# Crossed halves of a complex state scan, multiplied by VectorE out of PSUM instead of exchanged by transfers

## The chip, the cores and the metric

The kernel runs on one core of a Trainium2 chip. A core has five engines with their own instruction streams: TensorE (PE in the profile; its weight loads are listed as PEld), VectorE (DVE), ScalarE (ACT), GpSimd (POOL) and SyncE (SP). Each executes its stream in order and waits on semaphores that other engines and transfers set. Transfers (DMAs) are issued by SP, ACT or POOL, each into its own queue, and are carried out by 16 DMA engines that all queues share. SBUF is the on-chip memory of 128 partitions, PSUM the memory into which TensorE writes; it has 8 banks of 128 x 512 numbers in float32.

The metric is the device time of one execution in microseconds (us), as the median of the timed runs.

## The reference

One decoder layer on 1024 tokens of width 1024: a SwiGLU feed-forward half step, a mixer, a second feed-forward half step and a final norm, with shifts, scales and gates that come from a conditioning vector. The change lies in the mixer, in the part that the reference calls `s5_mixer`:

```python
lam_bar = jnp.exp(lam * dt)
b_bar = ((lam_bar - 1) / lam)[..., None] * b
bu = jnp.einsum('gpc,bsgc->bsgp', b_bar, uf.astype(jnp.complex64))
a = jnp.broadcast_to(lam_bar, bu.shape)
_, states = lax.associative_scan(_ssm_combine, (a, bu), axis=1)
y = jnp.einsum('gcp,bsgp->bsgc', c, states).real + d_skip * uf
y = jax.nn.gelu(y)
y = y * jax.nn.sigmoid(y @ glu_w + glu_b)
```

There are 32 groups of 16 channels, each with 64 complex states; `lam_bar` is a complex decay for each state. The mixer's other half is a gated convolution of three taps; both halves are normed and go through one output projection.

## The kernel before

Large products are done in float32 as three passes on TensorE (a high part and a low part of either factor; the product of the two low parts is dropped), by the helper `mm3`: three matmuls of 128 x 512. Weights arrive as tiles `raw` over SP's queue (sums of two blocks get their second summand by a transfer from POOL's queue); ACT casts each to its high part and DVE subtracts to get the low part, into tiles `w`, of which there are four. The large projections use a seven-product scheme (`seven`), each of whose seven steps has 8 calls of `mm3`, so a projection has 56. Three of its PSUM sums (A, B, C), each as a pair, live in six banks (`mm_ps`); DVE adds them up, and a bank comes free when DVE or ACT has read it.

**The order of the work.** The program is written as one stream in which `mm3` advances a clock by one tick, and side work is put on the clock: `clock.after(n, fn)` runs `fn` n ticks later. A planner then sets the order within each engine from this, so that two neighbours of the text may change places; in the stage of the batches below (`InOrder.strict`) the order is that of the text.

**The scan in complex numbers.** The time axis of 1024 is folded: 8 steps (TAU) are taken together by matrix products, and 128 folded steps (J) remain for the scan. The 32 groups are worked through in NB = 8 batches of GB = 4. For a batch a tile of 128 x 512 holds the real parts of the 64 states in partitions 0 to 63 and the imaginary parts in 64 to 127, with 4 x 128 folded steps along the row. Since the decay has a phase, the state is turned back by an angle before the scan, so that the scan itself has a real factor (`r8`), and turned forward after it. A turn is a complex product: `co` (cosines) times the tile, plus `si` (sines with signs) times the tile with its halves exchanged. Per batch (all in the mixer's stage):

- `state_in`: PE forms `px`, the input to the states (weights `mi` times `u`), in a bank of the six, and `py`, the direct part of the output (weights `mk` times `u`), in one of two further banks (`sm_ps`). ACT copies `px` to `X` (sX in the profile), and the helper `swapped` writes `X` with its halves exchanged into a tile (swx) by two transfers on ACT's queue.
- `state_scan`, 12 ticks later: DVE forms co times X and si times swx, adds them, runs four scans, and forms si times X and co times X.
- `state_swap`, at tick 20: two more transfers exchange the halves of si times X (into swz).
- `state_end`, at tick 31: DVE adds swz.
- `outputs`, at tick 34: PE adds the states' part (weights `mo`) to `py`, ACT applies the Gelu (yg), and ACT's queue stores the result (`y_d`).

A batch starts every 18 ticks, so that before the change two batches overlap: `outputs` of batch b at 34 lies two ticks ahead of `state_in` of batch b + 2 at 36.

`u_load` fetches a batch's u on ACT's queue from `u_d`, where the input projection's four parts have been stored by SP; `in_loads`, `mo_load`, `co_load` and `si_load` fetch the weights and tables on SP's queue. `mi`, `mk` and `mo` have one buffer, `u`, `co` and `si` two. After the scan `y_back` reads the results back as rows of channels, `x_again` fetches the residual stream, `split_g` splits the results for the gate `glu`, and `w_out` is the output projection; its first half needs `oa`, the normed convolution (`outnorm`), its second the gated results.

Beside the scan run the seven-step projections that the convolution needs, `cv0` and `cv2`, and `b`: 168 ticks in all. Their sums, the three-tap convolution (`conv`, five instructions for 128 channels) and the weights' low parts are DVE's other work in this stage.

**The batches' weights** are formed much earlier, in the first feed-forward half step (`ssm_batch`, as side work): DVE forms `cl` and `bl` by `comb` (two products with broadcast factors and a sum), PE forms `kp` and transposes `bl` into `tp`, ACT copies that to `mi`, and SP stores the tiles to DRAM (`mo_d`, `co_d`, `si_d`, `mk_d`, `mi_d`). These tiles come from one pool of four buffers (`bt`), so that the next batch's first instructions (`bb`) wait until stores have landed. Before the change `bl` has its columns in the order group, channel, step, so that DVE writes them at a stride of 8 numbers.

Of the kernel before, what the change touches and what calls it, by code (L numbers as in the profile page):

```python
# [13 lines left out]
F32 = mybir.dt.float32  # L14
# [7 lines left out]
P = 128  # L22
# [20 lines left out]
NB = 8  # L43
# [188 lines left out]
def hymba_layer(ctx: ExitStack, tc, x_d, xt_d, wm1_d, wmod_d, gu1_d, gs1_d, ds10_d, ds11_d, wl1_d, win_d, wcvb_d, wout_d, glu_d, gu2_d, gs2_d, wd2_d, ds20_d, ds21_d, ds22_d, wl2_d, cols_d, cond_d, lam_d, bc_d, out_d):  # L232
# [29 lines left out]
    def ps(name):  # L262
        return mm_ps.tile([P, HALF], F32, tag="mm", name=name)
# [942 lines left out]
    def ssm_batch(b):  # L1206
        bp = bps[0]
        gs = slice(b * GB, (b + 1) * GB)
        prm = ssm["prm"]
        bb = bp.tile([P, 2, GB, CH], F32, tag="bb", name=f"bb{b}")  # L1210
        q = tuple(ssm["q"][:, i, gs].unsqueeze(2).to_broadcast([P, GB, CH]) for i in range(2))
        cmul(bp, bb[:], prm[:, 0:2], q, [GB, CH], f"bb{b}")
        p1, p2, e1, e2 = ssm["tabs"]
        yield

        def bt(name):
            return bp.tile([P, 576], F32, tag="bt", name=name, bufs=4)

        def comb(dst, n, lam, src, op, nm):

            t = bt(nm)[:, : GB * n * CH].rearrange("p (g n c) -> p g n c", g=GB, n=n)
            la = [a[:, 0:n, gs].rearrange("p n g -> p g n").unsqueeze(3).to_broadcast([P, GB, n, CH]) for a in lam]
            sc = [a.unsqueeze(2).to_broadcast([P, GB, n, CH]) for a in src]
            V.tensor_tensor(out=dst, in0=la[0], in1=sc[0], op=ALU.mult)
            yield
            V.tensor_tensor(out=t, in0=la[1], in1=sc[1], op=ALU.mult)
            yield
            V.tensor_tensor(out=dst, in0=dst, in1=t, op=op)
            yield

        cl = bt(f"cl{b}")
        cl4 = cl[:].rearrange("p (g n c) -> p g n c", g=GB, n=9)
        yield from comb(cl4, 9, (p1, p2), (prm[:, 2], prm[:, 3]), ALU.add, f"clt{b}")
        SP.dma_start(mo_d[b].rearrange("p (g m) -> p g m", g=GB), cl4[:, :, 1:9, :].rearrange("p g n c -> p g (n c)"))
        if b + 1 < NB:
            prm_load(b + 1)
        bl = bt(f"bl{b}")
        bl4 = bl[:, :512].rearrange("p (g c n) -> p g n c", g=GB, n=8)
        yield from comb(bl4, 8, (e1, e2), (bb[:, 0], bb[:, 1]), ALU.add, f"blt{b}")

        def v3(a):
            return a[:, :512].rearrange("p (g m i) -> p g m i", g=GB, m=8)

        bs = [a[:, gs, :].unsqueeze(2).to_broadcast([P, GB, 8, 16]) for a in ssm["base"]]
        st = [ssm["step"][:, i, :, gs].rearrange("p m g -> p g m").unsqueeze(3).to_broadcast([P, GB, 8, 16]) for i in range(2)]
        r, t = bt(f"rot{b}"), bt(f"rott{b}")
        V.tensor_tensor(out=v3(r), in0=st[0], in1=bs[0], op=ALU.mult)
        yield
        V.tensor_tensor(out=v3(t), in0=st[1], in1=bs[1], op=ALU.mult)
        yield  # L1250
        V.tensor_tensor(out=r[:, :512], in0=r[:, :512], in1=t[:, :512], op=ALU.add)
        yield

        kp = sm([CH, 512], f"kp{b}")
        for g in range(GB):
            T.matmul(
                kp[:, g * P : (g + 1) * P], lhsT=bl4[:, g, 7, :], rhs=cl4[:, g, 0:8, :].rearrange("p n c -> p (n c)"), start=True, stop=True
            )
        tp = sm([P, 512], f"tp{b}")
        for g in range(GB):  # L1260
            T.transpose(tp[:, g * P : (g + 1) * P], bl[:, g * P : (g + 1) * P], ident[:])
        A.activation(t[64:128, :512], r[64:128, :512], AF.Copy, scale=-1.0)
        for half in (slice(0, 64), slice(64, 128)):
            SP.dma_start(co_d[b, half], r[0:64, :512])
        SP.dma_start(si_d[b, 0:64], r[64:128, :512])
        SP.dma_start(si_d[b, 64:128], t[64:128, :512])
        yield
        kc = bt(f"kc{b}")
        kc3 = kc[:CH, :512].rearrange("p (g m) -> p g m", g=GB)
        A.copy(kc[:CH, :512], kp[:])  # L1270
        mi = bt(f"mi{b}")
        A.copy(mi[:, :512], tp[:])
        yield
        for g in range(GB):
            V.scalar_tensor_tensor(
                out=kc3[:, g, 0:CH], in0=ident[:CH, :CH], scalar=ssm["lam"][:CH, 3, b * GB + g : b * GB + g + 1], in1=kc3[:, g, 0:CH], op0=ALU.mult, op1=ALU.add
            )
        for g in range(GB):
            SP.dma_start(mk_steps(b * GB + g), kc3[:, g, :].unsqueeze(1).to_broadcast([CH, TAU, P]))
        SP.dma_start(mi_d[b], mi[:, :512])  # L1280
        yield

    def gate1():
# [278 lines left out]
    def u_groups(b):  # L1562

        half = slice(b % 2 * GB * CH, (b % 2 + 1) * GB * CH)
        return u_d[b // 2][half, :].rearrange("(g c) (t j) -> (c t) g j", g=GB, t=TAU)
# [4 lines left out]

    def u_load(b):
        held["u", b] = sp.tile([P, GB, J], F32, tag="u", name=f"ub{b}", bufs=2)
        A.dma_start(held["u", b][:], u_groups(b))

    def co_load(b):
        held["co", b] = ld("co", co_d[b], b, 2)
# [1 line left out]
    def si_load(b):  # L1578
        held["si", b] = ld("si", si_d[b], b, 2)
# [5 lines left out]
    def mo_load(b):  # L1585
        held["mo", b] = ld("mo", mo_d[b], b)

    def swapped(src, b, nm):

        sw = sp.tile([P, GB * P], F32, tag=nm, name=f"{nm}{b}")  # L1590
        A.dma_start(sw[0:64], src[64:128])
        A.dma_start(sw[64:128], src[0:64])
        return sw

    def state_in(b):

        u, mi, mk = (held.pop((n, b)) for n in ("u", "mi", "mk"))
        px = ps(f"px{b}")
        py = held["py", b] = sm([P, GB * J], f"py{b}")
        for g in range(GB):  # L1600
            q = slice(g * P, (g + 1) * P)
            T.matmul(px[:, q], lhsT=mi[:, q], rhs=u[:, g, :], start=True, stop=True)
        X = held["X", b] = sp.tile([P, GB * J], F32, tag="sX", name=f"sX{b}")
        A.copy(X[:], px[:])
        held["sw", b] = swapped(X, b, "swx")
        for g in range(GB):
            q = slice(g * P, (g + 1) * P)
            T.matmul(py[:, q], lhsT=mk[:, q], rhs=u[:, g, :], start=g == 0, stop=False, skip_group_check=True)
        if b + 2 < NB:
            clock.after(3, lambda: u_load(b + 2))  # L1610
        if b + 1 < NB:
            clock.after(3, lambda: in_loads(b + 1))

    def state_scan(b):

        co, si, X, sw = held["co", b], held["si", b], held.pop(("X", b)), held.pop(("sw", b))
        V.tensor_tensor(out=X[:], in0=co[:], in1=X[:], op=ALU.mult)
        V.tensor_tensor(out=sw[:], in0=si[:], in1=sw[:], op=ALU.mult)
        V.tensor_tensor(out=X[:], in0=X[:], in1=sw[:], op=ALU.add)
        for g in range(GB):  # L1620
            q = slice(g * P, (g + 1) * P)
            V.tensor_tensor_scan(
                out=X[:, q], data0=r8[:, b * GB + g : b * GB + g + 1].to_broadcast([P, J]), data1=X[:, q], initial=0.0, op0=ALU.mult, op1=ALU.add
            )
        V.tensor_tensor(out=si[:], in0=X[:], in1=si[:], op=ALU.mult)
        V.tensor_tensor(out=co[:], in0=X[:], in1=co[:], op=ALU.mult)

    def state_swap(b):
        held["sw", b] = swapped(held.pop(("si", b)), b, "swz")
        if b + 2 < NB:  # L1630
            clock.after(13, lambda: si_load(b + 2))

    def state_end(b):
        co = held["co", b]
        V.tensor_tensor(out=co[:], in0=co[:], in1=held.pop(("sw", b))[:], op=ALU.add)

    def outputs(b):
        st, py, mo = (held.pop((n, b)) for n in ("co", "py", "mo"))
        for g in range(GB):
            late, early = slice(g * P + 1, (g + 1) * P), slice(g * P, (g + 1) * P - 1)  # L1640
            T.matmul(py[:, late], lhsT=mo[:, g * P : (g + 1) * P], rhs=st[:, early], start=False, stop=True, skip_group_check=True)
        yg = sp.tile([P, GB * J], F32, tag="yg", name=f"yg{b}")
        A.activation(yg[:], py[:], AF.Gelu_apprx_tanh)
        A.dma_start(y_groups(b), yg[:].rearrange("p (g j) -> p g j", g=GB))
        if b + 1 < NB:
            clock.after(3, lambda: mo_load(b + 1))
        if b + 2 < NB:
            clock.after(3, lambda: co_load(b + 2))
# [15 lines left out]
        for i in range(4):  # L1664
            clock.after(2 * i, lambda i=i, h=h: actG[h].append(split_act(yb[i][:, hsl(h)], f"yg{i}_{h}")))

    STEPS = (0, state_in), (12, state_scan), (20, state_swap), (31, state_end), (34, outputs)
    for b in range(NB):
        for n, step in STEPS:
            clock.after(6 + 18 * b + n, lambda b=b, step=step: step(b))  # L1670
    last = 6 + 18 * (NB - 1) + 34
    for i in range(4):
        clock.after((122, 128, 144, last + 10)[i], lambda i=i: y_back(i))

# [302 lines left out]
```

## Time and profile before

| | us |
|---|---|
| median of three timed runs | 1691.73 |
| lowest and highest | 1690.86, 1696.42 |
| the profiled execution's own time | 1698.34 |
| span of the profiled execution, first to last instruction | 1696.6 |
| mean granted TensorE clock in it, as a share of full speed | 0.983 |

A row of the windows view gives a stretch of the span (start and end in us from its start), its length, the time in which each engine was busy with the number of its instructions, the granted TensorE clock as a share of full speed, the share of time in which the DMA engines were busy, and GB/s. Where only PE is asked for, the other engines are left out. A row of waits gives who waited, for whom, the time in us in total, how often, and the longest. A row of the timeline gives the start, the duration, the engine, the operation, what it writes and reads with shapes, how many were merged, and in brackets the idle time before it and what ended it. A row of a tile's or the groups' view gives count, durations in ns (lowest, median, highest), first and last start, and shapes; the groups' view has busy us, mean ns of one, and the idle time before. A row of DMA issues has the queue, the count, the size of one and the median us from issue to landing.

### The profile page before, as it was taken

What the parts mean: (1) busy time and instruction counts of PE and PEld (TensorE: products, weight loads), DVE (VectorE), ACT (ScalarE), POOL (GpSimd) and SP (SyncE); (2) the same over time, 40 slices, a digit from 0 to 9 for tenths busy, and PEclk for the clock granted to TensorE, in tenths of its full rate; (3) what the DMA queues carried; (4) which work ended last, traced back from release to release, by engine and by line L of the source; (5) the groups of instructions that cost most, each with busy time, mean ns of one, the idle gap of its engine ahead of it and who ended that gap; (6) DMA issues with size and microseconds to landing.
All of it is one profiled execution on the core that took longest, in us unless ns stands there. A gap on an engine that the chain in (4) does not pass through costs nothing.

```text
span 1696.6 us, 20644 instructions
## 1 busy us (share of the span) xinstructions
PE 1651.6 (97%) x7437; PEld 1362.2 (80%) x7437; DVE 1135.4 (67%) x1683; ACT 725.8 (43%) x1080; POOL 183.2 (11%) x223
## 2 busy tenths in 40 slices
PE   8999999989999999998989999999999999999998
PEld 5888888868878888777867888888888888888887
DVE  7984587868566767774766787856655565444576
ACT  6654333333454341552323446534444444322345
POOL 2010100000010102100000022001000110100104
PEclk9999999999999999999989999999999999999999
DMA  9476699988987767466764813557888778889832
GB/s 351 134 169 190 172 266 253 259 241 255 275 235 223 175 217 240 173 211 167 208 181 138 299 43 125 148 119 216 223 237 234 203 219 235 262 283 307 249 77 100
DMA packets 134648, 352.64 MB, mean 208 GB/s; under 512 B 17553, under 2 KB 41361, under 8 KB 133522
## 3 DMA queue, kind: packets, MB, share of 16 engines
q1 hardware_dynamic: 108178, 276.87, 46.1%
q0 software_dynamic: 18432, 66.07, 22.9%
q10 hardware_dynamic: 7936, 8.39, 1.7%
q8 instruction: 58, 0.95, 0.2%
q14 instruction: 44, 0.36, 0.1%
HBM read 261.75 MB, written 76.94 MB: 200 GB/s over the span
## 4 chain that ended last, share of the span: by engine, by line
PE 65%; DMA 5%; DVE 5%; ACT 2%; issue 1%; POOL 1%; ACTq 0%; SPq 0%; DVEq 0%; POOLq 0%
PE wo L113 5%; PE fald L113 3%; PE fbd_1B L113 3%; PE fbd_0B L113 3%; PE fad_1B L113 2%; PE fad_0B L113 2%; DMA swx<-sX 2%; PE fbd_1C L113 1%; PE fbd_0C L113 1%; PE u L113 1%; PE gl L113 1%; PE fb0d L113 1%; PE fad_1C L113 1%; PE fad_0C L113 1%; PE fb10d L113 1%
## 5 line engine op out<-in xcount | busy, mean ns | idle before, releaser
L113 DVE TENSOR_TENSOR w<-raw,w 128x1024 fp32r<-128x1024 f32 (+1 forms) x256 | 308.9, 1207 | 249.4 <-ACT w L113 243.4
L113 ACT CAST w<-raw 128x1024 fp32r<-128x1024 f32 (+1 forms) x256 | 266.0, 1040 | 311.4 <-DMA raw<-in_ds 58.6
L175 POOL DMA_DIRECT2D raw<-in_gs x80 | 70.4, 883 | 741.0 <-DVE w L113 453.4
L113 DVE CUSTOM_DVE_ANT_0 wm<-wm,cact 128x1024 f32<-128x1024 f32 x56 | 72.4, 1309 | 4.0 <-DMA wm<-in_wmod 4.0
L175 POOL DMA_DIRECT2D raw<-in_ds x36 | 31.5, 875 | 311.9 <-DVE w L113 177.3
L113 PE MATMUL p<-h,w 128*128 128x512 f32 x192 | 49.4, 407 | 1.7 <-ACT h L113 1.5
L113 PE MATMUL wo<-oa,w 128*128 128x512 f32 x192 | 47.4, 407 | 3.4 <-ACT oa L113 3.4
L113 PEld LDWEIGHTS wo<-oa,w 128*128 128x128 f32 x192 | 37.5, 197 | 11.9 <-ACT oa L113 3.9
L113 PE MATMUL wo<-ob,w 128*128 128x512 f32 x192 | 45.0, 392 | 0.0
L113 PE MATMUL u<-h,w 128*128 128x512 f32 x192 | 44.5, 391 | 0.0
L113 PEld LDWEIGHTS p<-h,w 128*128 128x128 f32 x192 | 35.7, 192 | 9.9 <-ACT h L113 2.0
L113 PEld LDWEIGHTS u<-h,w 128*128 128x128 f32 x192 | 35.8, 188 | 7.7 <-DVE h L113 0.4
L113 PEld LDWEIGHTS wo<-ob,w 128*128 128x128 f32 x192 | 35.7, 188 | 7.6 <-DVE ob L113 0.3
L113 DVE TENSOR_TENSOR sX<-co,sX 128x512 f32<-128x512 f32 x8 | 5.5, 690 | 35.5 <-DMA swx<-sX 26.8
L175 POOL DMA_DIRECT2D raw<-in_wcvb x12 | 10.6, 880 | 170.2 <-DVE w L113 128.2
L113 PE MATMUL fb0u<-h,w 128*128 128x512 f32 x96 | 23.7, 391 | 0.0
L113 PE MATMUL fb0g<-h,w 128*128 128x512 f32 x96 | 23.2, 389 | 0.0
L113 PE MATMUL fald<-fa9lA,w 128*128 128x512 f32 x96 | 22.8, 391 | 0.0
L113 PE MATMUL gl<-yg,w 128*128 128x512 f32 x96 | 22.7, 392 | 0.0
L113 PE MATMUL fald<-fa0lA,w 128*128 128x512 f32 x96 | 22.4, 389 | 0.0
L113 PE MATMUL fald<-fa10lA,w 128*128 128x512 f32 x96 | 22.4, 389 | 0.0
L113 PE MATMUL py<-ub,mk 128*128 128x128 f32 x64 | 11.5, 336 | 10.7 <-ACT yg L113 10.7
(1663 smaller groups left out, 4096.7 us busy)
## 6 DMA issues: line engine op xcount, KB each, us to landing
raw<-in_gs SPq DMA_DIRECT2D x80, 512.0 KB, 4.5
raw<-in_gs POOLq DMA_DIRECT2D x80, 512.0 KB, 6.4
wm<-in_wmod SPq DMA_DIRECT2D x56, 512.0 KB, 6.6
raw<-in_ds SPq DMA_DIRECT2D x32, 512.0 KB, 4.8
raw<-in_ds POOLq DMA_DIRECT2D x32, 512.0 KB, 7.7
mw<-in_wm SPq DMA_DIRECT2D x8, 1024.0 KB, 8.3
raw<-in_wcvb SPq DMA_DIRECT2D x12, 512.0 KB, 4.3
raw<-in_wcvb POOLq DMA_DIRECT2D x12, 512.0 KB, 7.1
```

Of the source, the lines that this page charges most:

```text
L113: r = getattr(self.engine, name)(*args, **kw)
L175: self.G.dma_start(out=r, in_=src, accum_op=ALU.add)
```

## The change

- DVE takes the products of crossed halves itself: for each half of the partitions, one instruction reads `si` on the half that it writes and `px` on the other half, straight out of PSUM; after the scan, one instruction per half reads `X` and `si` on one half and writes the other. The copy of `px` by ACT and the four transfers of a batch go.
- The steps are called at other ticks: `state_turn` at 2, `state_scan` at 7, `state_back` at 10, `outputs` at 17; what follows the scan is tied to the new last tick.
- The loads of u and the stores of the results go from ACT's queue to SP's.
- `bl` is written in the order group, step, channel, without a stride; the transposed weights then have their rows in the order step, channel, and the store to `mi_d` puts them back in the order channel, step.

```diff
-        bl4 = bl[:, :512].rearrange("p (g c n) -> p g n c", g=GB, n=8)
+        bl4 = bl[:, :512].rearrange("p (g n c) -> p g n c", g=GB, n=8)
...
-        SP.dma_start(mi_d[b], mi[:, :512])
+        SP.dma_start(
+            mi_d[b].rearrange("(c n) m -> n c m", n=TAU), mi[:, :512]
+        )
...
-        A.dma_start(held["u", b][:], u_groups(b))
+        SP.dma_start(held["u", b][:], u_groups(b))
...
-    def swapped(src, b, nm):
-
-        sw = sp.tile([P, GB * P], F32, tag=nm, name=f"{nm}{b}")
-        A.dma_start(sw[0:64], src[64:128])
-        A.dma_start(sw[64:128], src[0:64])
-        return sw
+    LOW, HIGH = slice(0, 64), slice(64, 128)
...
-        px = ps(f"px{b}")
+        px = held["px", b] = ps(f"px{b}")
...
-        X = held["X", b] = sp.tile([P, GB * J], F32, tag="sX", name=f"sX{b}")
-        A.copy(X[:], px[:])
-        held["sw", b] = swapped(X, b, "swx")
...
+    def state_turn(b):
+
+        co, si, px = held["co", b], held["si", b], held.pop(("px", b))
+        X = held["X", b] = sp.tile([P, GB * J], F32, tag="sX", name=f"sX{b}")
+        sw = sp.tile([P, GB * J], F32, tag="sw", name=f"swx{b}")
+        V.tensor_tensor(out=X[:], in0=co[:], in1=px[:], op=ALU.mult)
+        for to, of in ((LOW, HIGH), (HIGH, LOW)):
+            V.tensor_tensor(out=sw[to], in0=si[to], in1=px[of], op=ALU.mult)
+        V.tensor_tensor(out=X[:], in0=X[:], in1=sw[:], op=ALU.add)
+
     def state_scan(b):
...
-        V.tensor_tensor(out=X[:], in0=co[:], in1=X[:], op=ALU.mult)
-        V.tensor_tensor(out=sw[:], in0=si[:], in1=sw[:], op=ALU.mult)
-        V.tensor_tensor(out=X[:], in0=X[:], in1=sw[:], op=ALU.add)
+        X = held["X", b]
...
-        V.tensor_tensor(out=si[:], in0=X[:], in1=si[:], op=ALU.mult)
+
+    def state_back(b):
+
+        co, si, X = held["co", b], held.pop(("si", b)), held.pop(("X", b))
+        sw = sp.tile([P, GB * J], F32, tag="sw", name=f"swz{b}")
+        for to, of in ((LOW, HIGH), (HIGH, LOW)):
+            V.tensor_tensor(out=sw[to], in0=X[of], in1=si[of], op=ALU.mult)
         V.tensor_tensor(out=co[:], in0=X[:], in1=co[:], op=ALU.mult)
-
-    def state_swap(b):
-        held["sw", b] = swapped(held.pop(("si", b)), b, "swz")
+        V.tensor_tensor(out=co[:], in0=co[:], in1=sw[:], op=ALU.add)
         if b + 2 < NB:
-            clock.after(13, lambda: si_load(b + 2))
-
-    def state_end(b):
-        co = held["co", b]
-        V.tensor_tensor(out=co[:], in0=co[:], in1=held.pop(("sw", b))[:], op=ALU.add)
+            clock.after(5, lambda: si_load(b + 2))
...
-        A.dma_start(y_groups(b), yg[:].rearrange("p (g j) -> p g j", g=GB))
+        SP.dma_start(y_groups(b), yg[:].rearrange("p (g j) -> p g j", g=GB))
...
-    STEPS = (0, state_in), (12, state_scan), (20, state_swap), (31, state_end), (34, outputs)
+    STEPS = (0, state_in), (2, state_turn), (7, state_scan), (10, state_back), (17, outputs)
...
-    last = 6 + 18 * (NB - 1) + 34
+    last = 6 + 18 * (NB - 1) + 17
```

More of the change, by code (lines that the diff above doesn't have):

```diff
@@ L1612, in state_in @@
             clock.after(3, lambda: in_loads(b + 1))
+    def state_turn(b):
[6 more added lines that the diff above has]
+        V.tensor_tensor(out=X[:], in0=X[:], in1=sw[:], op=ALU.add)
     def state_scan(b):
-        co, si, X, sw = held["co", b], held["si", b], held.pop(("X", b)), held.pop(("sw", b))
-        V.tensor_tensor(out=X[:], in0=co[:], in1=X[:], op=ALU.mult)
-        V.tensor_tensor(out=sw[:], in0=si[:], in1=sw[:], op=ALU.mult)
-        V.tensor_tensor(out=X[:], in0=X[:], in1=sw[:], op=ALU.add)
+        X = held["X", b]
         for g in range(GB):
```

## The prediction

> **What bounds the kernel now.** I read the page first: busy time by engine, then who waited for whom on TensorE (PE) in the stage of the scan, then the granted clock in windows behind each of those waits.
>
> ```profile
> PE 1651.6 (97%) x7437; PEld 1362.2 (80%) x7437; DVE 1135.4 (67%) x1683; ACT 725.8 (43%) x1080; POOL 183.2 (11%) x223
> ...
> PE py L113 <- ACT yg L113: 10.7, 3, 5.5
> PE px L113 <- DMA ub<-u_d: 4.0, 1, 4.0
> PE cv2uB L113 <- DVE cv2uc L113: 3.6, 1, 3.6
> PE wo L113 <- ACT oa L113: 3.4, 1, 3.4
> ...
> 754.80:762.00 7.20, 7.17 (x28) 0.61 0.88 291
> 793.10:799.50 6.40, 6.39 (x22) 0.62 0.91 184
> 827.50:833.00 5.50, 5.43 (x21) 0.69 0.91 268
> 857.10:863.00 5.90, 5.90 (x16) 0.51 0.32 92
> 884.10:891.00 6.90, 6.90 (x22) 0.56 0.60 171
> 918.90:925.00 6.10, 6.10 (x16) 0.56 0.55 191
> ...
> 745.00:926.00 181.00, 159.24 (x732) 133.31 (x731) 112.59 (x176) 51.84 (x72) 9.71 (x11) 0.90 0.69 186
> ```
>
> PE is busy for 97% of the span, so only what keeps PE waiting, or slow, can be won. The four rows of waits are all of PE's waits between 740 and 930 us: 10.7 + 4.0 + 3.6 + 3.4 = 21.7 us, in six gaps. The six windows begin where the gaps end; PE is busy through each (second number), but the granted clock (the third) is 0.51 to 0.69 instead of 1, so a window of length L loses (1 - clock) x L: 2.81, 2.43, 1.71, 2.89, 3.04 and 2.68, together 15.6 us. The stage thus loses 37.3 us of 181, and a gap costs nearly twice what the row of waits says.
>
> Behind the gaps stands VectorE (DVE), which works in order and stands still for transfers:
>
> ```profile
> DVE sX L113 <- DMA swx<-sX: 26.8, 4, 9.5
> DVE co L113 <- DMA swz<-si: 7.7, 5, 2.9
> DVE sX L113 <- DMA co<-co_d: 5.2, 1, 5.2
> ...
> 783.71 0.69 DVE L113 TENSOR_TENSOR sX<-co,sX 128x512 f32<-128x512 f32 x1 [8.48 <-DMA swx<-sX]
> 790.10 1.05 ACT L113 CAST w<-raw 128x1024 fp32r<-128x1024 f32 x1 [9.49 <-DVE cv0gu L113]
> 793.11 2.08 PE L113 MATMUL py<-ub,mk 128*128 128x128 f32 x8 [5.47 <-ACT yg L113]
> ```
>
> Read the last three as one chain: DVE waits 8.48 us for the exchange swx, so the addition cv0gu queued behind it is late, ScalarE (ACT) waits 9.49 us for that, the Gelu (yg) queued behind it is late, and PE waits 5.47 us for the Gelu to give back a bank of py. The exchange is the root.
>
> **The change, part by part.**
>
> *The exchange goes.* The two gaps at 793 and 827, the one at 884 (all py behind yg), the one at 857 and the one at 918 are those I expect to lose. Two things remove them. First, DVE no longer stands for swx and swz (34.5 us). Second, the calendar: py has two banks; before, outputs of batch b came at tick 34 and state_in of b + 2, which claims its bank, at tick 36. Now outputs come at 17, so 19 ticks lie between. A tick, three 512-column matmuls, is 0.68 us: twelve start 2.72 us after the twelve before them.
>
> ```profile
> 766.20 2.88 PE L113 MATMUL cv0gC<-h2S,w 128*128 128x512 f32 x12
> 768.92 2.88 PE L113 MATMUL cv0uC<-h2S,w 128*128 128x512 f32 x12
> ...
> 845.53 8.34 DMA co<-co_d
> ...
> 916.24 0.69 DVE L113 TENSOR_TENSOR co<-co,swz 128x512 f32<-128x512 f32 x1 [1.59 <-DMA swz<-si]
> 918.23 1.28 ACT L113 CAST oa<-oat 128x512 fp32r<-128x512 f32 x2 [2.91 <-DVE oat L113]
> ```
>
> 19 ticks are 12.9 us, over twice the longest such wait (5.5). The gap at 857 comes from co landing 8.34 us after its issue: before, its load had 11 ticks (37 to 48), 7.5 us; now 18 (20 to 38), 12.2 us, more than 8.34. The gap at 918 comes from batch 7 ending just as the output projection begins: oat stands behind batch 7's last additions. Now the last batch ends at tick 149 where the three projections end at 168 (3 x 56), so oat finds DVE free. Removed: 10.7 + 3.6 + 3.4 = 17.7 us of waits and 2.43 + 1.71 + 2.89 + 3.04 + 2.68 = 12.75 us of slow clock, 30.4 us. What is late next on PE there is nothing that a row shows; ready matmuls of the projections follow.
>
> *What DVE gets.* Per batch six full products and sums become eight instructions of which four work on 64 partitions.
>
> ```profile
> L113 DVE TENSOR_TENSOR swx<-si,swx 128x512 f32<-128x512 f32 x8 | 5.5, 684 | 0.0
> L113 DVE TENSOR_TENSOR cv0gt<-cv0gt,cv0gA 128x512 f32<-128x512 f32 x1 | 0.7, 687 | 0.0
> L113 ACT COPY sX<-px 128x512 f32<-128x512 f32 x8 | 4.7, 585 | 12.5 <-PE px L113 6.0 <-DVE co L113 3.6 <-DVE w L113 2.4
> ...
> L113 ACT COPY kc<-kp x8: 558/572/578, 228.5 to 423.8; 16x512 f32<-16x512 f32 x8
> L113 ACT COPY mi<-tp x8: 568/570/572, 229.0 to 424.3; 128x512 f32<-128x512 f32 x8
> ```
>
> No row has DVE on 64 partitions, or crossing halves. ScalarE takes 572 ns for 16 partitions and 570 for 128, so I take the full 0.69 us for a half; the low end is half of it (no added time at all). A product that reads PSUM (cv0gA) takes 687 ns against 684 for one that does not, so px costs nothing more. Added: 2 x 0.69 x 8 = 11.0 us on DVE (low end 0); ACT loses 8 x 0.585 = 4.7 us of copies. DVE goes from 112.6 us busy in 181 to 123.6 in some 150, from 62% to 82%: it still hides beneath PE, and if it does not, see the first rival. [...]
>
> *The transfers moved from ACT's queue to SP's* (eight u loads, eight y stores).
>
> ```profile
> ub<-u_d ACTq DMA_DIRECT2D x8, 256.0 KB, 7.0
> mk<-mk_d SPq DMA_DIRECT2D x8, 256.0 KB, 7.8
> raw<-in_wcvb SPq DMA_DIRECT2D x10, 512.0 KB, 5.0
> ...
> SPq L113 <- DMA swz<-si: 34.4, 9, 9.1
> ```
>
> A load of the same size and row length on SP (mk) takes 7.8 us against 7.0, so I expect no other landing time. Six of the u loads have 33 ticks (22 us). The first stands in the gap at 754 (4.0 us + 2.8 of clock). On SP it comes among the four stores of u that wait for ACT: issued early and landed fast, the gap goes (-6.8 us); the stores stand 4 ticks (2.7 us) apart, so behind the last one it is issued two steps, 5.4 us, later, and the gap grows by as much. I take 0. A y store now holds SP until its Gelu is done, with loads of weights behind it; SP stood longer before for swz, so I take 0 again.
>
> *The wait that is new.* DVE's first product now waits for the px matmuls themselves, with the projections' additions queued behind it, which PE needs to get banks back. It stands 2 ticks (1.4 us) after state_in, inside which I expect the px matmuls to end, so I take 0. px keeps its bank, one of six, for those 1.4 us and three products (2.1 us), where ACT's copy let it go after 0.6: 2.9 us longer, while the projections ask for a new pair of banks every 8 ticks (5.4 us) at most.
>
> *The weights' order.* bl is written without a stride:
>
> ```profile
> L113 DVE TENSOR_TENSOR bl<-tab,bb x8: 1130/1135/1152, 215.9 to 410.8; 128x512 f32<-128x512 f32 x8
> L113 DVE TENSOR_TENSOR blt<-tab,bb x8: 667/686/692, 217.4 to 411.7; 128x512 f32<-128x512 f32 x8
> L113 DVE TENSOR_TENSOR bl<-bl,blt x8: 1070/1155/1176, 221.7 to 415.2; 128x512 f32<-128x512 f32 x8
> ...
> PE kp L113 <- DVE bl L113: 4.2, 1, 4.2
> ...
> DVE bb L113 <- DMA si_d<-rott: 9.8, 2, 8.0
> DVE bb L113 <- DMA si_d<-rot: 8.2, 3, 4.1
> ...
> mi_d<-mi SPq DMA_DIRECT2D x8, 256.0 KB, 4.3
> ```
>
> The two strided instructions should fall to blt's 0.69: 0.45 + 0.46 us less, 7.3 us of DVE over eight batches, between 200 and 430 us, where PE waits for it once (kp, 4.2 us). That wait began with the 8.0 us for a store, so 0.9 us earlier is all that a batch gains; I count 0, with up to 1 us. The store of mi keeps its rows of 2 KB and is only written in another order.
>
> **Sum.** The profiled execution took 1698.3 us (span 1696.6 and 1.7 around it); 1698.3 - 30.4 = 1667.9. The median of the timed runs is 1691.7, 6.6 below. If that difference lies in the gaps, which depend on landing times, the median falls only to 1667.9; if it lies elsewhere, to 1661.3. I take the middle, **1665 us**. The forecast's own range is 1655 (the gap at 754 goes as well, 1661.3 - 6.8) to 1675 (a third of the 30.4 returns as new short waits, each with its slow clock).
>
> **The rivals.**
>
> *VectorE becomes the bound.* For: 123.6 us of work in 150, in order; besides transfers it waited 12.1 us for ACT's casts, and 123.6 + 12.1 = 135.7 leaves under 15 us, less than 2 us a batch.
>
> ```profile
> DVE w L113 <- ACT w L113: 12.1, 4, 5.1
> ```
>
> Against: those waits are partly echoes of the exchange itself. If DVE comes late to the additions that free PE's banks, half of the 30.4 stays: 1665 + 15 = 1680.
>
> *The reordered store holds the batches up.* If the store of mi takes twice as long in its new order, 8.6 instead of 4.3 us, its buffer is free later, and DVE, which stood 18.0 us for such stores (the two bb rows), stands up to 7 x 4.3 = 30 us more. PE paid 4.2 us for 18.0; with as much again for the clock, 30 us cost 14: 1665 + 14 = 1679. Against: no bb row names mi_d. [...]
>
> *It doesn't do what it says.* Gelu, py and the banks still hang on an in-order ACT, and PE waits for other things at the same places: within 5 us of 1691.7.
>
> *Slower: SP's queue.* A y store holds SP until its Gelu is done, and the weights stand behind. PE uses one weight tile in 8 ticks, 5.4 us; with three tiles ready, 16 us ahead, less 5.0 (raw), 1.05 (cast) and, at twice 0.69, 1.4 (difference), some 9 us of holding cost nothing. Each us over it is one of PE, with some 2.5 of slow clock behind. To eat up 30.4 us, eight holds have to last 10.3 us or more; at 12 us each it is 8 x (3 + 2.5) - 30.4 = +13.6: 1705. Against: SP's waits for the exchange were 9.1 at the longest, and those go.
>
> **Chances.** Forecast 0.60; VectorE 0.18; the store 0.08; no effect 0.06; SP 0.08. Faster by over 0.3% (about 5 us, what a measurement of this kernel can tell from no change) 0.86, within it 0.06, slower 0.08. The range reaches from the forecast's low end, 1655, over VectorE's and the store's case to 1684; some 0.2 lies outside.
>
> **What would show it.** Right: no row of DVE waiting for a transfer between halves; PE's waits in the stage at about 4 us, most of it the first px, and the clock near 1 behind the other places; co and si never waited for; half products near 0.69 us. VectorE's rival: PE rows that name DVE, at banks of cv and b. The store: bb waiting for mi_d. SP: casts of w waiting for raw. Wrong altogether: rows of py waiting for yg as before, or halves that take well over 0.69 us.

## The result and the profile after

| | before | after |
|---|---|---|
| median of six timed runs, us | 1691.62 | 1679.64 |
| lowest and highest, us | 1689.19 to 1696.42 | 1674.53 to 1681.06 |
| the profiled execution's own time, us | 1698.34 | 1679.18 |
| its span, us | 1696.6 | 1677.3 |
| mean granted clock | 0.983 | 0.989 |

The ratio after to before is 0.9921, with an interval from 0.9902 to 0.9941: faster, by 12.0 us in the medians, where 26.7 were forecast. The sign and the range held; under half of the forecast gain arrived.

The page's first part of after, and its waits of PE between 690 and 960 us (who waited, for whom, us in total, times, longest):

```profile
PE 1642.3 (98%) x7437; PEld 1353.9 (81%) x7437; DVE 1142.2 (68%) x1699; ACT 723.3 (43%) x1072; POOL 182.3 (11%) x223
```

```profile
PE wo L113 <- DVE oa L113: 3.5, 2, 2.1
PE nAbst L113 <- DVE nAbq L113: 3.4, 1, 3.4
PE wo L113 <- ACT oa L113: 3.3, 1, 3.3
PE py L113 <- DVE co L113: 1.4, 2, 0.7
```

No row has py waiting for yg any more, nor px for ub, nor cv2uB for cv2uc. But three rows are new or as large as before, and all three lie behind the projections: two where the output projection (wo) begins, the third (wo behind ACT's oa, 3.3 us) some 30 us into it. They belong to `outnorm`, the norm of the convolution half: DVE forms oat, ACT casts it to oa (the high part), DVE subtracts for the low part, and the first output matmuls wait for both; nAbq are the squares of the second half of the tokens, nAbst their sum on PE.

To see where the time went, I take the start of one tile's matmuls in each stage, by tile (count, ns lowest/median/highest, first and last start). First before, then after:

```profile
L113 PE MATMUL cv0gB<-h,w x24: 389/389/389, 746.5 to 803.0; 128*128 128x512 f32 x24
L113 PE MATMUL buB<-h,w x24: 387/389/398, 868.0 to 915.1; 128*128 128x512 f32 x24
L113 PE MATMUL wo<-oa,w x192: 387/389/792, 918.9 to 978.5; 128*128 128x512 f32 x192
L113 PE MATMUL fb0g<-h,w x96: 389/389/389, 1039.2 to 1074.5; 128*128 128x512 f32 x96
```

```profile
L113 PE MATMUL cv0gB<-h,w x24: 389/389/389, 745.8 to 788.1; 128*128 128x512 f32 x24
L113 PE MATMUL buB<-h,w x24: 388/389/389, 843.9 to 885.5; 128*128 128x512 f32 x24
L113 PE MATMUL wo<-oa,w x192: 388/389/796, 890.9 to 959.4; 128*128 128x512 f32 x192
L113 PE MATMUL fb0g<-h,w x96: 389/389/389, 1019.6 to 1054.8; 128*128 128x512 f32 x96
```

| stretch, us | before | after | difference |
|---|---|---|---|
| start of the span to the first cv0gB | 746.5 | 745.8 | -0.7 |
| stage of the scan: first cv0gB to last buB | 168.6 | 139.7 | -28.9 |
| hand-over and mixer's end: last buB to first fb0g | 124.1 | 134.1 | +10.0 |
| first fb0g to the end of the span | 657.4 | 657.7 | +0.3 |

The sum is -19.3, the difference of the spans. So the stage of the scan gave no less than was forecast of it, and 10 us were lost right behind it. The windows of the two stretches, before and then after (start and end, length, PE busy, granted clock, DMA share, GB/s):

```profile
746.50:915.50 169.00, 150.64 (x705) 0.91 0.70 187
915.50:960.60 45.10, 41.70 (x184) 0.92 0.73 257
```

```profile
745.80:885.90 140.10, 138.68 (x713) 1.00 0.77 207
885.90:931.00 45.10, 34.90 (x130) 0.81 0.65 237
```

In the stage PE's idle time falls from 18.4 to 1.4 us, and the clock rises from 0.91 to 1.00. In the 45.1 us behind it the idle time grows from 3.4 to 10.2 us, and the clock falls from 0.92 to 0.81.

The timeline of after shows how this happens (start, duration, engine, operation; in brackets the idle time before it and what ended it):

```profile
883.09 1.40 DVE L113 SCALAR_TENSOR_TENSOR oat<-ya,cols,nAabc 128x512 f32<-128x512 f32 x2
...
885.12 0.63 ACT L113 ACTIVATE nAbq<-ya 128x512 f32<-128x512 f32 x1 [2.96 <-DVE ya L113]
887.83 0.63 ACT L113 ACTIVATE nAbq<-ya 128x512 f32<-128x512 f32 x1 [2.08 <-DVE ya L113]
888.36 1.03 ACT L113 CAST w<-raw 128x1024 fp32r<-128x1024 f32 x1
889.30 2.17 ACT L113 CAST oa<-oat 128x512 fp32r<-128x512 f32 x4
889.33 1.70 PE L113 MATMUL nAbst<-one,nAbq 128*128 128x1 f32 x8 [3.43 <-DVE nAbq L113]
...
894.62 9.47 PE L113 MATMUL wo<-oa,w 128*128 128x512 f32 x30 [2.11 <-DVE oa L113]
...
919.80 2.18 ACT L113 CAST yg<-yb 128x512 fp32r<-128x512 f32 x4
921.88 2.18 ACT L113 CAST oa<-oat 128x512 fp32r<-128x512 f32 x4
922.55 0.96 PE L113 MATMUL wo<-oa,w 128*128 128x512 f32 x3 [3.27 <-ACT oa L113]
```

Two oat are ready by 884.5, and ACT stands idle for 2.96 and 2.08 us around that time. Yet it casts none of them before 889.30: in its program the four casts of oa stand behind the squares nAbq, and the last of those needs the last sums of b. On PE nAbst, too, stands ahead of the output projection. Later the second half's casts of oa stand behind the casts of yg, the gate's input. The casts themselves are not slower than in before (616 against 622 ns in the median); the order is the reason, and the change moved it. With `last` 17 ticks smaller, `y_back(3)`, `x_again` and `split_g(0)` also run 17 ticks earlier. In before none of these ran until b was done.

### The profile page after: what moved, and what is told of

Read it like the earlier page. It is cut to its first block, busy times and chain, and to the rows that moved or that the text cites. A ratio compares the mean times of both kernels' runs of the same rounds, so it can differ in the third digit from the quotient of the medians.

```text
span 1677.3 us, 20625 instructions
## 1 busy us (share of the span) xinstructions
PE 1642.3 (98%) x7437; PEld 1353.9 (81%) x7437; DVE 1142.2 (68%) x1699; ACT 723.3 (43%) x1072; POOL 182.3 (11%) x223
## 4 chain that ended last, share of the span: by engine, by line
PE 69%; DVE 5%; DMA 3%; issue 1%; ACT 1%; POOL 1%; SPq 0%; DVEq 0%; POOLq 0%; ACTq 0%
PE wo L113 5%; PE fald L113 4%; PE fbd_1B L113 3%; PE fbd_0B L113 3%; PE fad_1B L113 2%; PE fad_0B L113 2%; PE u L113 2%; PE fbd_1C L113 1%; PE fbd_0C L113 1%; PE gl L113 1%; PE fad_1C L113 1%; PE fad_0C L113 1%; PE fb10d L113 1%; DVE w L113 1%; PE fb0d L113 1%
## 5 line engine op out<-in xcount | busy, mean ns | idle before, releaser
L175 POOL DMA_DIRECT2D raw<-in_ds x36 | 31.5, 875 | 312.2 <-DVE w L113 201.4
L113 ACT COPY wa<-wo 128x512 f32<-128x512 f32 x16 | 9.4, 589 | 37.5 <-PE wo L113 36.6
L113 PE MATMUL fb0g<-h,w 128*128 128x512 f32 x96 | 23.2, 389 | 0.0
L113 PEld LDWEIGHTS fb0g<-h,w 128*128 128x128 f32 x96 | 18.0, 188 | 3.8
```

Of the source, the lines that this page charges most:

```text
L113: r = getattr(self.engine, name)(*args, **kw)
L175: self.G.dma_start(out=r, in_=src, accum_op=ALU.add)
```

## The experiments

All times are medians; each ratio is to the kernel before, run on the same chip, with its interval.

| kernel | us | ratio |
|---|---|---|
| before, unchanged | 1693.58 | 0.9992 [0.9974, 1.0011] |
| after | 1679.64 | 0.9921 [0.9902, 0.9941] |
| after, all that follows the scan at its old ticks ("old tail") | 1661.62 | 0.981 [0.9786, 0.9833] |
| the same a second time | 1662.07 | 0.9821 [0.9789, 0.9853] |
| after, y_back(3) alone at its old tick | 1669.02 | 0.9865 [0.9844, 0.9886] |
| after, yb3 in the other pool | 1667.64 | 0.9857 [0.9821, 0.9894] |
| after, split_g(0) and x_again at their old ticks | 1671.64 | 0.9878 [0.9847, 0.991] |
| after, old ticks of the scan and old tail | 1668.12 | 0.9857 [0.9832, 0.9883] |
| before, ends of a batch four ticks sooner | 1678.94 | 0.9933 [0.9908, 0.9958] |
| after, u and y on ACT's queue | 1679.95 | 0.9926 [0.9904, 0.9947] |
| old tail, u and y on ACT's queue | 1664.22 | 0.9843 [0.9803, 0.9883] |
| after, old order of bl and mi | 1679.3 | 0.9928 [0.9903, 0.9954] |

### Put the tail back

```diff
-    last = 6 + 18 * (NB - 1) + 17
+    last = 6 + 18 * (NB - 1) + 34
```

> The changed kernel with one line put back: all that follows the scan (reading the results back, the residual stream, splitting the results) is tied to tick 166 again instead of 149. Theory 'place': the fourth results tile, read back 17 ticks earlier, and the split results take buffers of the pool of 20 that oa needs, so oa is cast only when projection b has ended; with the old ticks oa is cast before, the waits of wo and nAbst (10.2 us) and the slow clock behind them (some 4 us) mostly go, and the time falls from 1680 to 1668 to 1673. Rival 'load': VectorE, with 11 us more work, is late at the hand-over whatever the ticks; then 1680 within 3.

It took 1661.62 us, even under the span expected; a second run of it, beside others below, gave 1662.07.

> The version with the old tail a second time, beside tail_act on one chip: 1659 to 1664 if the first result of 1661.6 holds; over 1668 if that run was a lucky one.

The matmuls by tile of this second run, and its windows:

```profile
L113 PE MATMUL cv0gB<-h,w x24: 389/389/389, 743.3 to 785.6; 128*128 128x512 f32 x24
L113 PE MATMUL buB<-h,w x24: 389/389/397, 841.5 to 883.1; 128*128 128x512 f32 x24
L113 PE MATMUL fb0g<-h,w x96: 389/389/389, 1000.4 to 1035.7; 128*128 128x512 f32 x96
```

```profile
743.30:883.50 140.20, 138.82 (x714) 1.00 0.76 206
883.50:931.00 47.50, 47.50 (x218) 1.00 0.71 251
```

The stage takes 139.8 us, as in after (139.7). Last buB to first fb0g takes 117.3 us instead of 134.1: PE is busy for all of the 47.5 us behind the stage, at full clock. PE's waits there, 10.2 us in the three rows of after, are gone. Against before (124.1) the hand-over is now 6.8 us shorter instead of 10.0 longer. So the whole loss at the hand-over is the moved tail, and this version beats both kernels.

### Which part of the tail

One at a time: first the read-back of the last results alone goes back.

```diff
-        clock.after((122, 128, 144, last + 10)[i], lambda i=i: y_back(i))
+        clock.after((122, 128, 144, last + 27)[i], lambda i=i: y_back(i))
```

> The changed kernel with only the read-back of the fourth results tile at tick 176 as before; the residual stream and the split stay early. Theory 'place': the first gap (nAbst and wo behind oa of the first half, 6.9 us and the clock behind it) goes, the second (oa of the second half behind the split results, 3.3 us) stays: 1672 to 1676, between the changed kernel and the one with all the old ticks. Rival 'load': 1680 within 3.

It took 1669.02 us. The rows of nAbst and of wo behind DVE's oa shrink from 6.9 to 1.6 us, and the later wo behind ACT's oa (3.3 us) stays. This was the theory's picture, with a larger gain than it gave.

Why would a transfer into yb3 hold up the casts of oa? The pool movA has 20 buffers, and blocks of cv and b, the tiles of oa and yb all come from it. If the early yb3 takes the buffer that oa would have had, the same early transfer into another pool must do no harm:

```diff
-        yb.append(mov(f"yb{i}", dtype=F32)[:].rearrange("p a b -> p (a b)"))
+        yb.append(mov(f"yb{i}", "AAAB"[i], dtype=F32)[:].rearrange("p a b -> p (a b)"))
```

> After, with one thing changed: yb3, the last of the four tiles that y_back fills, comes from the other pool of large tiles (movB, 8 buffers) instead of the pool with 20 buffers that the blocks of cv and b and the tiles of oa share; it is fetched at the new, early tick as in after. 'Buffer' theory (the early y_back(3) takes a buffer that oa then lacks): the casts of oa for the first half of the tokens come before b has ended, PE no longer waits 3.5 us for DVE's oa nor 3.4 us for nAbq, only the later wo <- ACT oa of 3.3 us stays; time as with y_back moved back, 1667 to 1672. 'Queue' theory (the early y_back(3) holds SP or DMA engines, so that weights or tiles come late, whatever buffer it fills): waits and time as in after, 1676 to 1681.

It took 1667.64 us: the theory of the buffer holds, that of the queue falls. The load of yb3 did not come later for it: it is issued 4.6 us ahead of the start of the last buB (877.76 and 882.4 us), in after 4.7 us ahead (880.82 and 885.5). The timeline has the casts earlier than after's:

```profile
880.75 1.29 ACT L113 CAST oa<-oat 128x512 fp32r<-128x512 f32 x2 [1.70 <-DVE oat L113]
...
882.63 5.38 PE L113 MATMUL wo<-oa,w 128*128 128x512 f32 x22
...
884.48 1.28 ACT L113 CAST oa<-oat 128x512 fp32r<-128x512 f32 x2 [1.83 <-DVE oat L113]
...
909.91 0.96 PE L113 MATMUL wo<-oa,w 128*128 128x512 f32 x3 [3.27 <-ACT oa L113]
```

The first two casts of oa run right behind their oat, ahead of the last squares, and wo begins without a wait. The order within ACT is fixed before the kernel runs, so the reading is this: with one tile less in movA at that point the planner has a buffer for oa sooner, and sets the casts ahead of the squares. That the pool decides is shown by the run; how the planner comes to its order is not. The second gap, at 909.91, is untouched, as the theory said.

Then the gate's side of the tail alone:

```diff
-    clock.after(last + 13, x_again)
-    clock.after(last + 22, lambda: split_g(0))
+    clock.after(last + 30, x_again)
+    clock.after(last + 39, lambda: split_g(0))
```

> After, with split_g(0) and x_again at their old ticks (188 and 179 instead of 171 and 162), y_back(3) at its new one. 'Place' theory (two separate causes): the first gap stays (wo <- oa and nAbst <- nAbq, some 5 to 7 us of waits at the start of the output projection), the second goes (no wo <- ACT oa of 3.3 us, since oa of the second half comes ahead of yg again); 1671 to 1676. Rival (one cause, y_back alone; the second gap is its echo): both gaps stay, 1677 to 1681.

It took 1671.64 us, and the waits of PE in the same stretch are these:

```profile
PE nAbst L113 <- DVE nAbq L113: 3.4, 1, 3.4
PE wo L113 <- DVE oa L113: 2.1, 1, 2.1
PE py L113 <- DVE co L113: 1.4, 2, 0.7
```

The first gap stays and the second goes: two separate causes. They add up: against after, the first is worth 10.6 and 12.0 us in its two runs, the second 8.0, and both together 18.0 and 17.6. In waits the first gap is 5.3 us (6.9 less the 1.6 that stay) and the second 4.7 (3.3 and 1.4), so each us of waiting is again worth some two, with the slow clock behind it (in after 0.73 from 885.9 to 904.7 and 0.62 from 922.0 to 931.0). These runs stem from chips on which before had medians of 1690.86 to 1693.1; with each kernel measured against the before of its own chip, the first gap is worth 12.1 and 11.2 us, the second 7.2, and both 19.5 and 16.8, so the sum still holds. Which of `x_again` and `split_g(0)` costs the second gap wasn't tried; the trace names the casts of yg, which are `split_g(0)`'s.

### The exchange or the calendar

The forecast had given two reasons for the five gaps. Each was tried alone. First the crossed products without the new calendar: all steps at their old ticks, with the old tail.

```diff
-    STEPS = (0, state_in), (2, state_turn), (7, state_scan), (10, state_back), (17, outputs)
+    STEPS = (0, state_in), (12, state_turn), (14, state_scan), (20, state_back), (34, outputs)
...
-            clock.after(5, lambda: si_load(b + 2))
+            clock.after(13, lambda: si_load(b + 2))
...
-    last = 6 + 18 * (NB - 1) + 17
+    last = 6 + 18 * (NB - 1) + 34
```

> The changed kernel's instructions (products of crossed halves, no exchange, SP's queue, the weights' order) at the ticks of before: turn at 12, scan at 14, back at 20, outputs at 34, and all that follows as before. Theory 'exchange': VectorE's standing for transfers was the root of TensorE's waits, so the waits of py for the Gelu stay away with the old ticks too: 1668 to 1676 (the hand-over has its old ticks). Rival 'calendar': outputs two ticks ahead of state_in of batch b + 2 was the root; py waits of 5 to 10 us come back and the time is 1682 to 1690.

```profile
PE wo L113 <- ACT oa L113: 3.4, 1, 3.4
PE cv2gB L113 <- DVE cv2gc L113: 1.4, 1, 1.4
```

It took 1668.12 us, 23.2 below before on that chip (1691.29). Without transfers inside a batch, py no longer waits for yg at all, though `outputs` still stand two ticks ahead of `state_in`. What stays are mainly the late last batch (wo behind oa, as in before) and cv2gB, a relative of the old gap at cv2uB, of which 0.4 us are left. The first px does not wait in this run either, so the 23.2 us probably hold the gap at 754 too, which belongs to neither reason.

Then the calendar without the crossed products: before, with a batch's last two steps four ticks sooner.

```diff
-    STEPS = (0, state_in), (12, state_scan), (20, state_swap), (31, state_end), (34, outputs)
+    STEPS = (0, state_in), (12, state_scan), (20, state_swap), (27, state_end), (30, outputs)
```

> The kernel before, with the exchange by transfers, but its last two steps four ticks earlier: end of the state at 27, outputs at 30, so six ticks instead of two lie ahead of state_in of batch b + 2. Theory 'exchange': VectorE still stands for swx and swz, some 30 us, and the time stays within 4 of 1691.6, with TensorE's waits moved rather than gone. Rival 'calendar': the py waits (10.7 us and 7 of clock) go: 1675 to 1683.

```profile
PE px L113 <- DMA ub<-u_d: 4.1, 1, 4.1
PE wo L113 <- ACT oa L113: 3.3, 1, 3.3
PE py L113 <- ACT yg L113: 3.1, 1, 3.1
...
PE cv2uB L113 <- DVE cv2uc L113: 0.8, 1, 0.8
```

It took 1678.94 us, 12.4 below before, while DVE still waited 21.3 us for swx and 13.6 for swz. Two of the three gaps of py are gone with room of six ticks. The theory of the exchange, which expected no more than 4 us from this run, missed here, as that of the calendar missed in the run before it. Either cause removed is worth much: 23 us for the exchange, 12 for these four ticks, and 28.8 to 31.5 for both with the old tail. They cover the same gaps, and are not to be added up.

### The queue of u and y

```diff
-        SP.dma_start(held["u", b][:], u_groups(b))
+        A.dma_start(held["u", b][:], u_groups(b))
...
-        SP.dma_start(y_groups(b), yg[:].rearrange("p (g j) -> p g j", g=GB))
+        A.dma_start(y_groups(b), yg[:].rearrange("p (g j) -> p g j", g=GB))
```

> The changed kernel with the loads of u and the stores of the results on ScalarE's queue again. Theory 'queue is nothing': 1680 within 3, first px wait of 0 to 1 us. Rival 'queue': the wait of the first px for u (4.0 us, 6.8 with the clock) had gone because of the queue; it comes back and the time is 1684 to 1687.

It took 1679.95 us, after's time. Its trace has the first px waiting 4.0 us for ub again, but the medians show no price for it. The profiled execution shows one: from the first cv0gB (740.8) to the end of the stage (last buB, 886.2) it took 145.4 us where after took 139.7, but it reached the stage 5.0 us sooner. The same edit on the version with the old tail:

> The version with the old tail (all that follows the scan at its old ticks), with the loads of u and the stores of y on ACT's queue as before the change. 'Queue counts' theory: the first px waits 4 us for ub again with some 2.8 us of slow clock behind it, and nothing else in the stage can swallow that, so 6 to 7 us more than the old tail with SP's queue: 1666 to 1670. 'Queue is nothing' theory: PE makes up for the gap later, within 2.5 us of the old tail, 1659 to 1664.

It took 1664.22 us beside 1662.07, between the spans of the two theories and with overlapping runs (1661.92 to 1673.15 and 1659.58 to 1664.83), and its px does not wait. The issue of the load and the first px, after with ACT's queue and then the old tail with it:

```profile
737.12 0.39 ACTq L113 DMA_DIRECT2D ub<-u_d  x1
...
749.05 2.05 PE L113 MATMUL px<-ub,mi 128*128 128x128 f32 x8 [4.04 <-DMA ub<-u_d]
```

```profile
743.64 0.40 ACTq L113 DMA_DIRECT2D ub<-u_d  x1
...
751.59 1.05 PE L113 MATMUL px<-ub,mi 128*128 128x128 f32 x8
```

The same load took 11.9 us in the one execution and at most 8.0 in the other, from the same place in ACT's order. So with ACT's queue this gap comes in some executions and not in others. Of the profiled executions here, four of the five with u on ACT's queue have it (3.5 to 4.1 us), and none of the eight with u on SP's. What the queue is worth in the median stays open: 0.3 us between the one pair of runs, 2.2 between the other.

### The weights' order

```diff
-        bl4 = bl[:, :512].rearrange("p (g n c) -> p g n c", g=GB, n=8)
+        bl4 = bl[:, :512].rearrange("p (g c n) -> p g n c", g=GB, n=8)
...
-        SP.dma_start(
-            mi_d[b].rearrange("(c n) m -> n c m", n=TAU), mi[:, :512]
-        )
+        SP.dma_start(mi_d[b], mi[:, :512])
```

> The changed kernel with bl at a stride and the store of mi in plain order, as before. Theory 'hidden': VectorE gets 7.3 us more work between 200 and 430 us, beneath TensorE: 1680 within 2, with the wait of kp at 3 to 5 us. Rival 'store': the reordered store holds VectorE up; with the plain one the time falls by 4 or more, to 1676 or less, and bb waits less than the 18.1 us of the changed kernel.

It took 1679.3 us, after's time: the two edits, undone together, are worth nothing that shows. Nor is the one hiding the other: between 190 and 450 us PE waits 4.0 us in after and 4.5 in this run. The sign that was named for the store's rival, DVE's bb waiting for mi_d (7.8 us), shows only here, with the plain store; all of bb's waits for stores are 18.1 us in after and 24.4 here.

### The kernel before once more

> The kernel before, unchanged, for a second profile. Theory 'spread': its profiled execution of 1698.3 us was one with long landings; a second one lies near the median of 1691.6, with less than the 21.7 us of waits of TensorE in the stage of the scan (some 15 to 18). Rival 'profiling': a profile costs some 6 us in this kernel always: 1697 to 1699 again, with waits of 21 to 22.

Its profiled execution took 1696.0 us, its median was 1693.58, and its waits in the stage were py for yg 9.4 us, px for ub 3.5, wo for oa 3.4 and cv2uB for cv2uc 3.2: 19.5 us in the same six gaps, where the first profile had 21.7. The gaps are there in both executions, 2.2 us apart. Neither span that was expected was met, and what lay in the 6.6 us between the first profile and the median is only in part explained by that. That profiling always costs some 6 us is not borne out: the profiled executions of the other kernels lie between 2.5 us below and 3.1 us above their medians.

## Why the prediction was right and wrong

**The cause and its size in the stage: right.** Five gaps were to give 30.4 us, of which 6.1 (3.4 and 2.68) belong to the hand-over at 918 and 24.3 to the stage. The stage became 28.9 us shorter. That includes the gap at 754, 6.8 us, which was taken as unchanged and went; 24.3 + 6.8 = 31.1 makes 2.2 too much, of which 1.4 is the new wait of py for co. The clock is 1.00 through the stage, as the idea that each gap drags slow clock behind it requires. The windows of after agree: 0.81 where PE idled for 10.2 of 45.1 us and 1.00 where it idled for 1.4 of 140.1.

**The step that failed** stands at the end of the exchange's part: "Now the last batch ends at tick 149 where the three projections end at 168 (3 x 56), so oat finds DVE free", and "What is late next on PE there is nothing that a row shows". DVE was free: two oat were done by 884.5. Late next was ACT's cast behind it, for which the order left no place until b had ended. I had read the new `last` only as the end of the scan. It is also the date of `y_back(3)`, `x_again` and `split_g(0)`; the working names none of the three, though a step that is moved has to be priced with all that it takes along. yb3 took one of 20 buffers 17 ticks early, and 17 ticks early the casts of yg went ahead of those of oa. The kernel before could have raised the question: oa and yb have one pool, and by its row the gap at 918 was already one of wo behind oa. The forecast of 6.1 us saved at the hand-over turned into 10.0 lost. With the tail put back, 6.8 are saved.

**The sum.** With the old tail the kernel runs at 1661.62 and 1662.07 us, within the 1661.3 to 1667.9 that the sum gave. But this version has lost the gap at 754 too, which the sum left in; with its 6.8 us taken off, the sum gives 1654.5 to 1661.1, and the runs lie just above that. What the forecast described is close to this version; the change as it was made lost 18 us of it. Against the sum's 1667.9 the profiled execution of after came some 11 us late: 16.1 at the hand-over (6.1 were to be saved, 10.0 were lost), less 4.6 that the stage gave beyond its 24.3.

**What was taken as nothing.** The half products cost the full time, as assumed (686 to 687 ns), and reading px in PSUM costs nothing that shows (687 against 686 ns). The wait that is new, DVE's product for px, is there (5.1 us in four waits, at 765.89, 780.84, 810.97 and 857.77) and no row of PE waits behind it: the two waits of py for co, 1.4 us, stand at 839.33 and 855.00, in batches whose px DVE did not wait for. DVE has no wait for a transfer left between 740 and 890 us, as the forecast's sign of being right required. Rows of after, by tile (ns lowest/median/highest):

```profile
L113 DVE TENSOR_TENSOR swx<-si,px x16: 683/687/691, 751.6 to 859.8; 64x512 f32<-64x512 f32 x16
L113 DVE TENSOR_TENSOR swz<-sX,si x16: 684/686/690, 755.2 to 863.3; 64x512 f32<-64x512 f32 x16
L113 DVE TENSOR_TENSOR sX<-co,px x8: 679/688/689, 750.9 to 857.8; 128x512 f32<-128x512 f32 x8
L113 DVE TENSOR_TENSOR bl<-tab,bb x8: 681/686/691, 216.1 to 409.7; 128x512 f32<-128x512 f32 x8
```

swx reads PSUM and swz does not: 687 against 686 ns, on crossed halves, and the same as on 128 partitions (688 for sX from px, 686 for bl). bl fell to 686 ns, as forecast, and was worth 0, as forecast.

**The rivals.** *VectorE as the bound* fell. The window of after from the first cv0gB to the first wo (busy time of PE, PEld, DVE, ACT and POOL, each with its count):

```profile
745.80:891.00 145.20, 140.35 (x722) 119.09 (x720) 121.68 (x186) 46.84 (x64) 8.85 (x10) 0.99 0.77 207
```

DVE is busy for 121.68 of 145.20 us, 84% where 82% were forecast, and inside the stage only py behind co, 1.4 us, names it. *The reordered store* fell with the run that undid it. That the store of mi takes twice its 4.3 us, the term from which the rival's 1679 was worked out, is shown by no run: the trace of after has no landing time for this store, but no wait of bb there names mi_d, and bb's waits for stores are 18.1 us between 200 and 430 us, where before had 19.7. *SP's queue* fell too. ACT's casts of w wait for raw, the sign named for it, but only for 3.8 us between 740 and 900 us (2.1 in before), and no row of PE waits for w. The longest hold by a Gelu was within the 9 us that the prediction had called free, by the waits of SP in after:

```profile
SPq L113 <- DVE swz L113: 28.2, 6, 8.1
SPq L113 <- PE py L113: 22.9, 8, 6.1
SPq L113 <- ACT yg L113: 9.1, 4, 8.2
```

*That it doesn't do what it says* fell with the stage. The time that came out, 1679.64, is that of two of these rivals, 1680 and 1679, but neither of their mechanisms was at work beyond those 1.4 us. The agreement is luck, and so is it that the time lies within the range, which reached past 1675 only for these two rivals.

**The offset.** The profile of before lay 6.6 us above its median, and half of that was taken off. After's profile lies 0.5 us below its median, so the profiles differ by 19.2 us and the medians by 12.0. Why the gap of before's profile was so large stays open.

## What to carry to other kernels

When a stage becomes shorter, list everything that is dated from its end, with the buffers and the places in the engines' orders that it takes; a single early transfer into a shared pool cost 10.6 to 12.0 us here, and nothing in its own row looked late. Two causes of one gap are not to be added: removing either was worth 23 and 12 us, and both some 30. And a forecast whose time comes out near a rival's has not thereby met the rival: the stages have to be compared one by one. And look at the hand-over behind the stage with the same care as at the stage, since the engine that was relieved (DVE) may not be the one that comes next in the chain (ACT).

## What the runs showed of the hardware

A DVE product on 64 partitions that reads the other 64, from SBUF or PSUM, took 686 to 687 ns for a row of 512 in after, as on 128 partitions (688 for sX from px, 686 for bl). A load of 256 KB from the same place in ACT's order took 11.9 us in one execution and at most 8.0 in another, which decides here whether PE stands for 4 us.
